# Seven products instead of eight in the input projection, and a multiplication moved to ScalarE

## The chip, the cores and the metric

The kernel runs on one core of one Trainium2 chip. The metric is the device time of one execution in microseconds (us). TensorE (PE) multiplies matrices, VectorE (DVE) and ScalarE (ACT) work on elements, SyncE (SP) issues most of the transfers (DMA). All data are float32. Products on PE take their operands in two parts, `hi` (the value rounded to a shorter format, fp32r) and `lo` (the rest); one product of two numbers is then three products on PE: hi x hi, hi x lo, lo x hi.

## What is computed

Two layers of an encoder with 256 tokens of width 2048. Per layer, cut to what matters here:

```
h = rmsnorm(x, norm_g[l])
proj = h @ w_in[l]                       # 2048 -> 7168 columns
a_x, a_b, a_c, a_g, d_q, d_k, d_v, d_g, m_q, m_g = split(proj)
q = rmsnorm(d_q per head half of 64)     # differential attention, 6 heads
k = rmsnorm(d_k per head half of 64)
v = d_v;  the attention's output is gated by silu(d_g)
...                                      # gated convolution (a_*), cross-attention (m_*)
x = x + concat(y_A, y_D, y_M) @ w_out[l]
```

## The kernel before

The 256 tokens are two row halves of 128 (`NT` = 2). The normalised, transposed input stands in SBUF as `xT`, hi and lo, in 16 row tiles of 128 (`KT`). A projection is worked off in blocks of 512 columns (`NB`). `block` (L308) holds two accumulators in PSUM, one for each row half, and walks the 16 row tiles in chunks of two (`CK`). For a chunk `load_w` (L284) loads 2 x 128 x 512 weights into a `raw` tile (L291, SP's queue), ACT casts `hi` (L294), DVE subtracts `lo` (L295). `products` (L298, L305) then makes 2 row tiles x 2 row halves x 3 parts = 12 products on PE. Four `raw`, four `hi` and four `lo` tiles go round, so the preparation of a chunk can run three chunks ahead of its products. The PSUM has four banks for accumulators (two blocks), two with the tag `s` and two with the tag `t`.

The six blocks of the differential attention begin at column `C_D`: blocks 0 to 2 are queries and keys, blocks 3 to 5 values and gates. Layer 0 takes them in the order 0 to 5. Layer 1 begins blocks 3 and 0 with the first 12 row tiles, ends them when the last quarter of the new x is there, and goes on with 1, 2, 4, 5. After each of blocks 0 to 2 `normed_steps` (L427) makes the norm's factors: squares on ACT (L436), sums on DVE (L437), an inverse square root as a chain of small DVE steps (`rsqrt`, L192), and then one DVE multiplication for each row half that writes the scaled block into a sheet (L445). The sheet is turned by DVE (L481) and carried through DRAM by DMA.

Work beside the blocks is written as generators. `run_side` counts the chunks and steps each generator when its count has come; `later(g, n)` starts one n chunks on. The order of an engine's instructions is made when the program is built, by a scheduler that puts each as early as its inputs allow, in the order of the program where several are ready. `pin` (`keep_in_program_order`) ties an instruction behind the one that the program issued just before it on the same engine.

In the output projection a scheme with seven products is already used, for two blocks of 512 columns at once and a pair of row tiles. `token_sums` (L353) makes four sums of token tiles on DVE, with their hi and lo. `seven` (L368) loads two rows of tiles of 1024 columns into `wide` tiles (L373), makes sums and differences of weights on DVE (L380) and their hi and lo (L377), and makes seven products of three parts each (L351): into the accumulators of the `near` and the `far` block, and into four more banks `x1`, `x5`, `x6`, `x7` (tags `s` and `t`). `collect` adds these up on DVE when the last pair has been made (L1247, L1251). Layer 0 has two such pairs there, layer 1 three.

Of the kernel before, what the change touches and what calls it, by code (L numbers as in the profile page):

```python
# [10 lines left out]
F32 = mybir.dt.float32  # L11
F32R = mybir.dt.float32r
I32 = mybir.dt.int32
AF = mybir.ActivationFunctionType
ALU = mybir.AluOpType
# [3 lines left out]
P = 128  # L19
# [3 lines left out]
NT = SEQ // P  # L23
# [6 lines left out]
HALF = 64  # L30
MH = W_MEM // P
EPS = 1e-6
NB = 512
CK = 2
PARTS = 8
SPLIT = 3
B = 32
NA = P // B
PAIR_EVERY = 9
QT = NB // P  # L40
# [3 lines left out]
C_D = 3072  # L44
# [4 lines left out]
def encoder(ctx: ExitStack, tc: tile.TileContext, x, mem, norm_g, w_in, conv_w, conv_b,  # L49
            dq_g, dk_g, lq1, lk1, lq2, lk2, head_g, mem_norm_g, w_mem_kv, mq_g, mk_g, w_out, out):  # L50
    nc = tc.nc
# [9 lines left out]
    keep = pool("keep", 1)  # L61
# [9 lines left out]
    def nm(s):  # L71
        uid[0] += 1
        return f"{s}_{uid[0]}"
# [140 lines left out]
    def later(g, n):  # L214
        due[id(g)] = chunk[0] + n
        return g
# [55 lines left out]

        return w[k * P:(k + CK) * P].rearrange("(j p) c -> p j c", p=P)

    def x_row_tiles(w, k):

        q, j = divmod(k, QT)
        return w[q * NB:(q + 1) * NB].rearrange("(p j) c -> p j c", j=QT)[:, j:j + CK]

    def raw_tile():  # L280
        return wp.tile([P, CK, NB], F32, tag="raw", name=nm("raw"), bufs=4)
# [16 lines left out]
    def accumulators():  # L298
        return [ps_acc.tile([P, NB], F32, tag="acc", name=nm("acc")) for _ in range(NT)]
# [53 lines left out]
    def token_sums(stat, k, home):  # L353

        f = tmp.tile([P, 2, SEQ], F32, tag="nat", name=nm("f"), bufs=3)
        pin(nc.vector.tensor_tensor(f, stat[:, 0, k:k + 2, :].bitcast(F32), stat[:, 1, k:k + 2, :].bitcast(F32), ALU.add))
        a11, a21, a12, a22 = f[:, 0, 0:P], f[:, 0, P:SEQ], f[:, 1, 0:P], f[:, 1, P:SEQ]
        s = tmp.tile([P, 4, P], F32, tag="nat", name=nm("sums"), bufs=3)
        yield 1
        pin(nc.vector.tensor_tensor(s[:, 0], a21, a22, ALU.add))  # L360
        pin(nc.vector.tensor_tensor(s[:, 2], a11, a21, ALU.subtract))
        pin(nc.vector.tensor_tensor(s[:, 1], s[:, 0], a11, ALU.subtract))
        pin(nc.vector.tensor_tensor(s[:, 3], a12, s[:, 1], ALU.subtract))
        yield 1
        pin(nc.scalar.copy(home[:, 0], s))
        pin(nc.vector.tensor_tensor(home[:, 1], s, home[:, 0].bitcast(F32), ALU.subtract))

    def seven(stat, k, sums, w, col0, c_near, c_far, x, first, last, homes, meanwhile):  # L368


        a, b = (pl.tile([P, 2, NB], F32, tag=tag, name=nm("wide")) for pl, tag in homes)
        for j, raw in enumerate((a, b)):
            pin(nc.sync.dma_start(raw.rearrange("p j c -> p (j c)"), w[(k + j) * P:(k + j + 1) * P, col0:col0 + 2 * NB]))  # L373

        def split(src, to=None):
            hi, lo = to or parts_tiles()
            return ((hi, pin(nc.scalar.copy(hi, src))), (lo, pin(nc.vector.tensor_tensor(lo, src, hi.bitcast(F32), ALU.subtract))))  # L377

        def minus(dst, v, u):
            pin(nc.vector.tensor_tensor(dst, v, u, ALU.subtract))  # L380

        def side_of(parts, j):
            return [v[:, j] for v, _ in parts]

        one = keep.tile([P, 2, 1, NB], F32R, tag="mga", name=nm("one"))
        b11 = split(a[:, 0:1], (one[:, 0], one[:, 1]))
        minus(a[:, 0], a[:, 1], a[:, 0])
        minus(a[:, 1], b[:, 1], a[:, 1])
        b2 = split(b)
        minus(b[:, 1], b[:, 1], a[:, 0])  # L390
        minus(b[:, 0], b[:, 0], b[:, 1])
        meanwhile()
        t13 = split(a)
        t42 = split(b)

        def tokens(j, t):
            return [stat[:, part, k + j, t * P:(t + 1) * P] for part in range(2)]

        def summed(i):
            return [sums[:, part, i] for part in range(2)]  # L400

        x1, x5, x6, x7 = x
        product(tokens(0, 0), x1, side_of(b11, 0), first, last)
        product(tokens(1, 0), c_near[0], side_of(b2, 0), False, False)
        product(summed(3), c_far[0], side_of(b2, 1), first, False)
        product(summed(0), x5, side_of(t13, 0), first, last)
        product(summed(2), x7, side_of(t13, 1), first, last)
        product(tokens(1, 1), c_near[1], side_of(t42, 0), False, False)
        product(summed(1), x6, side_of(t42, 1), first, last)
# [20 lines left out]
    def normed_steps(vec, acc, gs, st, home):  # L430

        ng = NB // gs
        ss = small.tile([P, NT, ng], F32, tag=f"ss{ng}", name=nm("ss"))
        for t in range(NT):
            sq = tmp.tile([P, NB], F32, tag="nat", name=nm("sq"), bufs=3)
            nc.scalar.activation(sq, acc[t], AF.Square)  # L436
            vec.tensor_reduce(ss[:, t], sq.rearrange("p (g d) -> p g d", d=gs), AX.X, ALU.add)  # L437
            vec.tensor_scalar(ss[:, t], ss[:, t], col(st, R2_64 if gs == HALF else R2_128, t), EPS,
                              ALU.mult, ALU.add)
        r = rsqrt(ss.rearrange("p t g -> p (t g)"), NT * ng, vec).rearrange("p (t g) -> p t g", t=NT)  # L440
        both = home()
        for t in range(NT):
            vec.tensor_scalar(r[:, t], r[:, t], col(st, R, t), None, ALU.mult)
            w = min(gs // B, NA)
            vec.tensor_tensor(  # L445
                both[:, :, :, t].rearrange("p (g b) j c -> p j g b c", b=w),
                acc[t].rearrange("p (j g b c) -> p j g b c", g=NA // w, b=w, c=B),
                r[:, t].rearrange("p (j g) -> p j g", g=NA // w).unsqueeze(3).unsqueeze(4)
                .to_broadcast([P, NB // P, NA // w, w, B]), ALU.mult)
        return both  # L450

    def normed(acc, gs, st, home):
# [595 lines left out]
    for l in range(DEPTH):  # L1048
# [8 lines left out]
        def x_block(cols, order=ALLK, **how):  # L1057
            return block(xT, w_in[l], cols, order, rows=x_row_tiles, **how)

        def begin_pair(n, p):  # L1060
            tasks.append(later(p, max(1, start + round(PAIR_EVERY * n) - chunk[0])))


        order = range(6) if l == 0 else (3, 0, 1, 2, 4, 5)
        begun = {b: x_block([(C_D + b * NB, NB)], ALLK[:-QT], more=True) for b in order[:2]} if l > 0 else {}
        for b in order:
            if b in begun:
                acc = x_block([(C_D + b * NB, NB)], ALLK[-QT:], acc=begun[b])
            else:
                acc = x_block([(C_D + b * NB, NB)], ready=m.ready if l == 0 and b == order[0] else None)  # L1070
            if b == 3:
                v = keep.tile([P, NT, W_DIFF], F32, tag="v", name=nm("v"))
                ga = keep.tile([P, NT, W_DIFF], F32, tag="ga", name=nm("ga"))
            if b == 4:
                start = chunk[0]
                for n in range(DH // 2):
                    begin_pair(n + n // 2 * 2 / 3, pair((2 * n, 2 * n + 1), (lambda heads: diff_scores(l, heads, yT),
                                                                 lambda h, s: diff_weights(l, h, s)),
                                       (lambda h, yn, po, iv: diff_out(h, yn, po, iv, st, ga),
                                        lambda h, y: split_T(yT, CG + h, y, hgain[:, l:l + 1], pin=True)), v))  # L1080
            if b < 3:
                tasks.append(later(qk_T(l, yT, normed(acc, HALF, st, sheets(("mqT", "mga", "e")[b])),
                                 (0, 0, 4) if b == 0 else (0, 4, 2) if b == 1 else None,
                                 (256, 0, 2) if b == 1 else (0, 2, 4) if b == 2 else None), 8))
            else:
                for t in range(NT):
                    if b == 3:
                        nc.scalar.activation(v[:, t, 0:NB], acc[t], AF.Copy, scale=col(st, R, t))
                    elif b == 4:
                        nc.scalar.activation(v[:, t, NB:768], acc[t][:, 0:256], AF.Copy, scale=col(st, R, t))  # L1090
                        silu2(ga[:, t, 0:256], acc[t][:, 256:512], st, t)
                    else:
                        silu2(ga[:, t, 256:768], acc[t], st, t)
# [172 lines left out]

        def pair_at(n):
            def run(near):
                seven(yT, paired[n], sums[n], w_out[l], 2 * NB, near, far, x, n == 0, n == len(paired) - 1,
                      homes[n], (lambda: leave(1, accs[1], pin, 4)) if n == 0 else lambda: None)  # L1270
                if n == len(paired) - 1:
                    tasks.append(later(collect(near), 5))
                run_side(1)
            return run
# [36 lines left out]
```

## Time and profile before

| what | value |
|---|---|
| median of 3 runs | 918.87 us (918.57 to 920.05) |
| profiled execution | 919.19 us |
| its span (first to last instruction) | 917.4 us |
| granted clock of TensorE | 1.00 |
| PE busy | 911.1 us, 99% |
| DVE busy | 712.2 us, 78% |
| ACT busy | 492.8 us, 54% |

A row of a group reads: line, engine, operation, output<-inputs, shapes, count | busy time in us, mean of one in ns | idle time of the engine just before them, and what ended it. A row of a timeline begins with the start and the duration in us and ends, in brackets, with the idle time before it and its releaser. Matmuls overlap, so their busy time says little; the distance of their starts does.

### The profile page before, as it was taken

The page shows a single profiled execution, that of the slowest core. Times are in us where ns is not written, and L with a number is a line of the kernel's source. Part 1 is how long each engine was busy: PE and PEld are TensorE (multiplying, and loading weights), DVE is VectorE, ACT ScalarE, POOL GpSimd, SP SyncE. Part 2 cuts the span into 40 slices and gives each one's busy share as a digit, 9 for nine tenths or more (in the row PEclk, how much of TensorE's full clock was granted, in tenths as well). Part 3 has the DMA queues.
Part 4 walks back from the last instruction along what each step waited for, and adds up shares of the span by engine and source line. Part 5 has one row for each costly group of instructions (what it writes and reads, how often), then busy time and mean ns, then how long its engine had stood idle before and what let it go on. Part 6 is the DMA issues. An engine that isn't in the chain of part 4 may idle for free.

```text
span 917.4 us, 12473 instructions
## 1 busy us (share of the span) xinstructions
PE 911.1 (99%) x4209; PEld 753.6 (82%) x4209; DVE 712.2 (78%) x1281; ACT 492.8 (54%) x770; POOL 38.2 (4%) x68
## 2 busy tenths in 40 slices
PE   8999999999999999999999999999999999999998
PEld 6888888888888888888888888888888888888887
DVE  5579978757789779587689857778888889488786
ACT  5667644445546556445556544456545546446352
POOL 2434010000000000000000000000000000000000
PEclk9999999999999999999999999999999999999999
DMA  8889888885786998989777867997887998978842
GB/s 288 287 245 251 283 247 232 250 235 179 205 235 172 263 273 248 234 248 255 242 220 227 277 196 216 267 243 182 237 223 187 249 268 258 257 227 246 280 155 92
DMA packets 244560, 215.16 MB, mean 235 GB/s; under 512 B 131976, under 2 KB 171720, under 8 KB 244496
## 3 DMA queue, kind: packets, MB, share of 16 engines
q1 hardware_dynamic: 239520, 208.71, 79.0%
q0 software_dynamic: 3776, 4.59, 2.1%
q10 hardware_dynamic: 1200, 1.07, 0.4%
q8 instruction: 33, 0.54, 0.2%
q14 instruction: 31, 0.25, 0.1%
HBM read 193.30 MB, written 21.00 MB: 234 GB/s over the span
## 4 chain that ended last, share of the span: by engine, by line
PE 98%; DMA 1%; SPq 0%; DVE 0%; ACT 0%; issue 0%; ACTq 0%
PE acc L305 91%; PE x L351 2%; PE po L519 1%; PE acc L351 1%; PE s L609 1%; DMA raw<-in_w_mem_kv_dram 1%; PE po L734 1%; PE pt L748 0%; SPq L818 0%; PE s L667 0%; PE s L666 0%; PE s L668 0%; SPq L881 0%; DVE lo L901 0%; DVE lo L295 0%; ACT hi L900 0%
## 5 line engine op out<-in xcount | busy, mean ns | idle before, releaser
L305 PE MATMUL acc<-hi,xT 128*128 128x512 f32 x1792 | 559.5, 390 | 0.0
L294 ACT CAST hi<-raw 128x1024 fp32r<-128x1024 f32 x270 | 283.1, 1052 | 292.3 <-PE acc L305 227.6
L295 DVE TENSOR_TENSOR lo<-raw,hi 128x1024 fp32r<-128x1024 f32 x270 | 328.7, 1220 | 134.8 <-ACT hi L294 133.2
L305 PEld LDWEIGHTS acc<-hi,xT 128*128 128x128 f32 x1792 | 336.2, 188 | 70.0
L305 PE MATMUL acc<-lo,xT 128*128 128x512 f32 x896 | 349.3, 390 | 0.4 <-DVE lo L295 0.4
L305 PEld LDWEIGHTS acc<-lo,xT 128*128 128x128 f32 x896 | 168.2, 188 | 34.3 <-DVE lo L295 0.8
L305 PE MATMUL acc<-hi,yT 128*128 128x512 f32 (+1 forms) x432 | 134.2, 388 | 0.0
L305 PEld LDWEIGHTS acc<-hi,yT 128*128 128x128 f32 x432 | 81.0, 188 | 16.7
L305 PE MATMUL acc<-lo,yT 128*128 128x512 f32 x216 | 83.7, 388 | 0.0
L305 PE MATMUL acc<-hi,memT 128*128 128x512 f32 x248 | 78.1, 393 | 0.0
L305 PEld LDWEIGHTS acc<-hi,memT 128*128 128x128 f32 x248 | 46.1, 188 | 9.5
L901 DVE SCALAR_TENSOR_TENSOR lo<-raw,cva,hi 128x1024 fp32r<-128x1024 f32 (+1 forms) x34 | 41.0, 1218 | 14.6 <-ACT hi L900 14.5
L305 PE MATMUL acc<-lo,memT 128*128 128x512 f32 x124 | 48.0, 391 | 0.3 <-DVE lo L901 0.2
L305 PEld LDWEIGHTS acc<-lo,yT 128*128 128x128 f32 x216 | 40.6, 188 | 8.4
L900 ACT ACTIVATE hi<-raw,cva 128x1024 fp32r<-128x1024 f32 (+1 forms) x34 | 36.5, 1099 | 12.1 <-DMA raw<-in_w_mem_kv_dram 11.9
L623 ACT ACTIVATE e<-e,mx 128x256 f32<-128x256 f32 x48 | 23.8, 497 | 8.4 <-DVE mx L619 8.4
L305 PEld LDWEIGHTS acc<-lo,memT 128*128 128x128 f32 x124 | 23.3, 188 | 6.0 <-DVE lo L901 1.1
L377 ACT CAST hi<-wide 128x1024 fp32r<-128x1024 f32 x15 | 15.5, 1049 | 16.3 <-DVE wide L380 6.8
L765 POOL DMA_DIRECT2D xt<-in_x_dram x32 | 21.4, 677 | 19.4 <-DVE rsy L189 13.9
L377 DVE TENSOR_TENSOR lo<-wide,hi 128x1024 fp32r<-128x1024 f32 x15 | 18.1, 1220 | 3.5 <-ACT hi L377 3.3
L481 DVE STREAM_TRANSPOSE sh<-sh 128x1024 f32<-128x1024 f32 (+2 forms) x14 | 17.3, 1237 | 0.0
L1166 ACT ACTIVATE sh<-acc,st 128x512 f32<-128x512 f32 (+1 forms) x16 | 8.9, 579 | 14.6 <-DMA d<-sh 11.7
(202 smaller groups left out, 713.2 us busy)
## 6 DMA issues: line engine op xcount, KB each, us to landing
raw<-in_w_in_dram SPq DMA_DIRECT2D x192, 512.0 KB, 4.7
raw<-in_w_out_dram SPq DMA_DIRECT2D x54, 512.0 KB, 4.7
raw<-in_w_in_dram SPq DMA_DIRECT2D x64, 256.0 KB, 4.1
raw<-in_w_mem_kv_dram SPq DMA_DIRECT2D x30, 512.0 KB, 6.2
d<-sh SPq DMA_DIRECT2D x88, 128.0 KB, 4.1
sh<-d SPq DMA_DIRECT2D x72, 128.0 KB, 4.3
wide<-in_w_out_dram SPq DMA_DIRECT2D x10, 512.0 KB, 6.6
xs<-in_x_dram SPq DMA_DIRECT2D x4, 512.0 KB, 6.5
```

Source lines behind the costliest of these rows:

```text
L294: nc.scalar.copy(hi, raw)
L295: nc.vector.tensor_tensor(lo_, raw, hi.bitcast(F32), ALU.subtract)
L305: i = nc.tensor.matmul(acc, left, right, start=start, stop=stop)
L351: nc.tensor.matmul(acc, left[a], right[b], start=first and i == 0, stop=last and i == 2)
L377: return ((hi, pin(nc.scalar.copy(hi, src))), (lo, pin(nc.vector.tensor_tensor(lo, src, hi.bitcast(F32), ALU.subtract))))
L481: tc.keep_in_program_order(nc.vector.transpose(src, src))
L519: nc.tensor.matmul(po[:, t, :], eT[:, i, t, k, :], v[:, k, h * P:(h + 1) * P], start=k == 0, stop=k == NT - 1)
L609: pin(nc.tensor.matmul(s[c][:, i, :], yT[rows, a, h, i * P:(i + 1) * P], yT[rows, b, CG + h, :], start=n == 0, stop=n == 2))
L623: nc.scalar.activation(e[:, c, i], e[:, c, i], AF.Exp, bias=mx[:, c, i:i + 1], accum_out=sm[:, c, i:i + 1])
L765: tc.keep_in_program_order(nc.gpsimd.dma_start(st[:, n], src[n * B:(n + 1) * B].rearrange("p (b r) -> b p r", b=NA)))
L900: both = (nc.scalar.activation(hi[:, j], raw[:, j], AF.Copy, scale=g), nc.vector.scalar_tensor_tensor(lo[:, j], raw[:, j], g, hi[:, j].bit ...
L901: nc.vector.scalar_tensor_tensor(lo[:, j], raw[:, j], g, hi[:, j].bitcast(F32), ALU.mult, ALU.subtract))
```

## The change

In each layer two blocks of w_in are made together with the scheme of seven products for some of their row tiles: blocks 3 and 4 in layer 0, with one pair of row tiles (0 and 1), put in after four chunks of block 3; blocks 1 and 2 in layer 1, with two pairs (row tiles 0 to 3), put in after three and after five chunks of block 1. The remaining row tiles of both blocks are made as before. `x_sums` makes the token sums of `xT`, in layer 0 right ahead of block 3, in layer 1 right after block 3. `collect` forms four sums `us` in SBUF from the banks of the x tiles, beginning directly behind the last pair, and `gather` adds the accumulators to them when a block ends; what follows reads `us` in place of the accumulators. Homes of new tiles are tags that exist. In blocks 0 to 2 of both layers the multiplication by the norm's factors (`gs == HALF`) goes from two DVE operations of 512 columns to sixteen ACT operations of 64 columns; that of the memory queries stays on DVE.

```diff
-    def x_row_tiles(w, k):
+    def x_row_tiles(w, k, n=CK):
         q, j = divmod(k, QT)
-        return w[q * NB:(q + 1) * NB].rearrange("(p j) c -> p j c", j=QT)[:, j:j + CK]
+        return w[q * NB:(q + 1) * NB].rearrange("(p j) c -> p j c", j=QT)[:, j:j + n]
...
-    def seven(stat, k, sums, w, col0, c_near, c_far, x, first, last, homes, meanwhile):
+    def seven(stat, k, sums, rows, c_near, c_far, x, first, last, homes, meanwhile, single=(keep, "mga")):
...
-            pin(nc.sync.dma_start(raw.rearrange("p j c -> p (j c)"), w[(k + j) * P:(k + j + 1) * P, col0:col0 + 2 * NB]))
+            pin(nc.sync.dma_start(raw.rearrange("p j c -> p (j c)"), rows(k + j)))
...
-        one = keep.tile([P, 2, 1, NB], F32R, tag="mga", name=nm("one"))
+        one = single[0].tile([P, 2, 1, NB], F32R, tag=single[1], name=nm("one"))
...
-            vec.tensor_tensor(
-                both[:, :, :, t].rearrange("p (g b) j c -> p j g b c", b=w),
-                acc[t].rearrange("p (j g b c) -> p j g b c", g=NA // w, b=w, c=B),
-                r[:, t].rearrange(...)..., ALU.mult)
+            to = both[:, :, :, t].rearrange("p (g b) j c -> p j g b c", b=w)
+            of = acc[t].rearrange("p (j g b c) -> p j g b c", g=NA // w, b=w, c=B)
+            if gs == HALF:
+                for at in range(ng):
+                    j, g = divmod(at, NA // w)
+                    nc.scalar.activation(to[:, j, g], of[:, j, g], AF.Copy, scale=r[:, t, at:at + 1])
+            else:
+                vec.tensor_tensor(to, of, r[:, t]..., ALU.mult)
...
+        def x_sums(n, tag):
+            home = keep.tile([P, 2, 4, P], F32R, tag=tag, name=nm("sums"))
+            for _ in token_sums(xT, 2 * n, home):
+                pass
+            return home
+
+        def joint(b, places, summed, home):
+            near, far = accumulators(), accumulators()
+            x = [pl.tile([P, NB], F32, tag=tag, name=nm("x"))
+                 for pl, tag in ((ps_s, "s"), (ps_s, "s"), (ps_t, "t"), (ps_t, "t"))]
+            u = keep.tile([P, 3, NB], F32, tag=home, name=nm("u"))
+            us = [u[:, 0], u[:, 1], u[:, 2], tmp.tile([P, NB], F32, tag="yn", name=nm("u"))]
...
+            def collect():
+                x1, x5, x6, x7 = x
+                pin(nc.scalar.copy(us[0], x1))
+                plus(us[2], us[0], x6)
+                plus(us[1], us[2], x7)
+                yield 1
+                plus(us[2], us[2], x5)
+                plus(us[3], us[1], x5)
+
+            def pair_at(n):
+                def run(near):
+                    rows = lambda k: x_row_tiles(w_in[l], k, 1)[:, 0, C_D + b * NB:C_D + (b + 2) * NB]
+                    seven(xT, 2 * n, summed[n], rows, near, far, x, n == 0, n == len(places) - 1,
+                          ((tmp, ("sh", "e")[n]),) * 2, lambda: None, ((tmp, "e"), (keep, "mga"))[l])
+                    if n == len(places) - 1:
+                        tasks.append(later(collect(), 1))
+                    run_side(1)
+                return run
+
+            x_block([(C_D + b * NB, NB)], ALLK[2 * len(places):], acc=near, opened=(False, False),
+                    between={c: pair_at(n) for n, c in enumerate(places)})
+            return near, far, us
+
+        def gather(acc, us):
+            for t in range(NT):
+                nc.vector.tensor_tensor(us[t], acc[t], us[t], ALU.add)
+            return us
...
+        near_b, far_b, places, tags, home = ((3, 4, (8,), ("bgx",), "bgT"), (1, 2, (6, 10), ("bgT", "mkT0"), "bgx"))[l]
+        far, summed = None, []
         for b in order:
             if b in begun:
                 acc = x_block([(C_D + b * NB, NB)], ALLK[-QT:], acc=begun[b])
+                if b == 3:
+                    for n in range(len(places)):
+                        summed.append(x_sums(n, tags[n]))
+            elif b == near_b:
+                if not summed:
+                    summed = [x_sums(n, tags[n]) for n in range(len(places))]
+                acc, far, us = joint(b, places, summed, home)
+                acc = gather(acc, us[0:2])
+            elif b == far_b:
+                acc = x_block([(C_D + b * NB, NB)], ALLK[2 * len(places):], acc=far, opened=(True, False))
+                acc = gather(acc, us[2:4])
             else:
```

More of the change, by code (lines that the diff above doesn't have):

```diff
@@ L444, in normed_steps @@
             w = min(gs // B, NA)
-            vec.tensor_tensor(
-                both[:, :, :, t].rearrange("p (g b) j c -> p j g b c", b=w),
-                acc[t].rearrange("p (j g b c) -> p j g b c", g=NA // w, b=w, c=B),
-                r[:, t].rearrange("p (j g) -> p j g", g=NA // w).unsqueeze(3).unsqueeze(4)
-                .to_broadcast([P, NB // P, NA // w, w, B]), ALU.mult)
+            to = both[:, :, :, t].rearrange("p (g b) j c -> p j g b c", b=w)
[5 more added lines that the diff above has]
+            else:
+                vec.tensor_tensor(to, of, r[:, t].rearrange("p (j g) -> p j g", g=NA // w).unsqueeze(3).unsqueeze(4)
+                                  .to_broadcast([P, NB // P, NA // w, w, B]), ALU.mult)
         return both
@@ L1058, in x_block, with plus @@
             return block(xT, w_in[l], cols, order, rows=x_row_tiles, **how)
+        def x_sums(n, tag):
[9 more added lines that the diff above has]
+            us = [u[:, 0], u[:, 1], u[:, 2], tmp.tile([P, NB], F32, tag="yn", name=nm("u"))]
+            def plus(dst, v, u):
+                pin(nc.vector.tensor_tensor(dst, v, u, ALU.add))
+            def collect():
[22 more added lines that the diff above has]
+            return us
         def begin_pair(n, p):
@@ L1268, in run @@
             def run(near):
-                seven(yT, paired[n], sums[n], w_out[l], 2 * NB, near, far, x, n == 0, n == len(paired) - 1,
+                seven(yT, paired[n], sums[n], lambda k: w_out[l][k * P:(k + 1) * P, 2 * NB:4 * NB], near, far, x, n == 0, n == len(paired) - 1,
                       homes[n], (lambda: leave(1, accs[1], pin, 4)) if n == 0 else lambda: None)
```

## The prediction

> **What bounds the kernel now.** I read the page's busy table first, then the groups of instructions, then the groups in the stretch that the change touches, then the timelines of VectorE (DVE) and ScalarE (ACT) there.
>
> ```profile
> span 917.4 us, 12473 instructions
> PE 911.1 (99%) x4209; PEld 753.6 (82%) x4209; DVE 712.2 (78%) x1281; ACT 492.8 (54%) x770; POOL 38.2 (4%) x68
> L294 ACT CAST hi<-raw 128x1024 fp32r<-128x1024 f32 x270 | 283.1, 1052 | 292.3 <-PE acc L305 227.6
> L295 DVE TENSOR_TENSOR lo<-raw,hi 128x1024 fp32r<-128x1024 f32 x270 | 328.7, 1220 | 134.8 <-ACT hi L294 133.2
> ...
> L305 PE MATMUL acc<-hi,xT 128*128 128x512 f32 x193 | 59.5, 389 | 0.0
> L305 PE MATMUL acc<-lo,xT 128*128 128x512 f32 x96 | 37.3, 389 | 0.0
> ```
>
> TensorE (PE) is idle for 917.4 - 911.1 = 6.3 us in all. The column behind the second bar shows who waits: ACT's cast of a weight chunk waits 227.6 us for PE to give back a `hi` buffer, and DVE's `lo` waits 133.2 us for ACT. Both helpers run ahead and PE sets the pace. The last two rows are the groups of PE between 549.6 and 614.9 us, three blocks of layer 1: 289 products in 65.3 us, one of them shared with the block before. So a product costs PE 65.3/288 = 0.2267 us (its 389 ns overlap the next), a chunk of two row tiles (12 products) 2.72 us, a block of eight chunks 21.8 us.
>
> How far do the helpers run ahead? These are rows of two timelines in the first block that would be paired, block 3 of layer 0; ACT's first, DVE's behind the dots:
>
> ```profile
> 163.16 1.28 ACT L436 ACTIVATE sq<-acc 128x512 f32<-128x512 f32 x2 [0.98 <-PE acc L305]
> 172.00 1.05 ACT L294 CAST hi<-raw 128x1024 fp32r<-128x1024 f32 x1 [1.66 <-PE acc L305]
> 174.72 1.05 ACT L294 CAST hi<-raw 128x1024 fp32r<-128x1024 f32 x1 [1.15 <-PE acc L305]
> ...
> 163.79 1.37 DVE L437 TENSOR_REDUCE ss<-sq 128x8 f32<-128x512 f32 x2 [0.36 <-ACT sq L436]
> 165.41 1.23 DVE L295 TENSOR_TENSOR lo<-raw,hi 128x1024 fp32r<-128x1024 f32 x1
> 167.65 1.23 DVE L295 TENSOR_TENSOR lo<-raw,hi 128x1024 fp32r<-128x1024 f32 x1
> 170.37 1.23 DVE L295 TENSOR_TENSOR lo<-raw,hi 128x1024 fp32r<-128x1024 f32 x1 [0.36 <-ACT hi L294]
> 171.78 1.28 DVE L445 TENSOR_TENSOR sh<-acc,rsy 128x512 f32<-128x512 f32 x2
> 173.09 1.22 DVE L295 TENSOR_TENSOR lo<-raw,hi 128x1024 fp32r<-128x1024 f32 x1
> ```
>
> A buffer given back at 172.00 holds a finished `lo` at 173.09 + 1.22 = 174.31. PE then still has three prepared chunks, until 172.00 + 3 x 2.72 = 180.16. The lead is 5.9 us: DVE may fall that far behind before PE feels it.
>
> **Part 1, the products removed.** A pair replaces 2 row tiles x 2 row halves x 2 blocks x 3 parts = 24 products by 7 x 3 = 21. Three pairs remove 9: 9 x 0.2267 = **2.04 us**, all on the path. No product is added elsewhere (sums and collecting are DVE's and ACT's), so this is the most that can be gained.
>
> **Part 2, what DVE gets.** The same scheme already runs five times on w_out, so its prices stand in rows by shape:
>
> ```profile
> L377 DVE TENSOR_TENSOR lo<-wide,hi 128x1024 fp32r<-128x1024 f32 x15 | 18.1, 1220 | 3.5 <-ACT hi L377 3.3
> L377 DVE TENSOR_TENSOR one<-wide,one 128x512 fp32r<-128x512 f32 x5 | 3.4, 683 | 0.0
> L380 DVE TENSOR_TENSOR wide<-wide 128x512 f32<-128x512 f32 x10 | 6.9, 692 | 0.3
> L356 DVE TENSOR_TENSOR f<-yT 128x512 f32<-128x512 f32 x5 | 3.4, 684 | 0.0
> L360 DVE TENSOR_TENSOR sums<-f 128x128 f32<-128x128 f32 x5 | 1.4, 284 | 0.0
> L366 DVE TENSOR_TENSOR sums<-sums,sums 128x512 fp32r<-128x512 f32 x5 | 3.4, 683 | 0.0
> L1247 DVE TENSOR_TENSOR u<-u,x 128x512 f32<-128x512 f32 x8 | 5.2, 676 | 0.1
> L445 DVE TENSOR_TENSOR sh<-acc,rsy 128x512 f32<-128x512 f32 x16 | 10.2, 681 | 0.0
> ```
>
> A pair: 3 x 1.220 + 0.683 + 4 x 0.692 = 7.11 us of DVE, in 21 x 0.2267 = 4.76 us of PE. The two ordinary chunks that it replaces cost 2 x 1.22. Token sums: 0.684 + 4 x 0.284 + 0.683 = 2.50 us a pair. Collecting and gathering: 8 additions of 0.676 a layer, 5.4 us. Given back: 12 multiplications of 0.681 (the 16 of the row less the four of the memory queries), 8.2 us. Sum over the kernel: 3 x (7.11 - 2.44 + 2.50) + 2 x 5.4 - 8.2 = +24 us of DVE, on 712.2 of 917.4. On average that is hidden; locally it may not be:
>
> ```profile
> 543.70:549.60 5.90, 5.90 (x28) 4.89 (x27) 2.91 (x3) 3.36 (x4) 0.00 (x0) 1.00 0.64 178
> 549.60:571.40 21.80, 21.80 (x97) 18.04 (x97) 15.82 (x29) 9.53 (x11) 0.00 (x0) 1.00 0.74 219
> 571.40:593.10 21.70, 21.70 (x97) 17.98 (x96) 16.86 (x30) 10.46 (x11) 0.00 (x0) 1.00 0.96 264
> 457.40:485.70 28.30, 28.30 (x125) 23.29 (x125) 25.54 (x29) 18.27 (x28) 0.00 (x0) 1.00 0.72 219
> ```
>
> Columns: stretch, length, busy PE, PEld, DVE, ACT, POOL, clock (1.00 throughout), DMA share and GB/s.
>
> *Layer 0* (one pair, after four chunks of block 3, which begins at T0 = 163.1). PE reaches the pair at T0 + 10.9. Its third product needs the sums at T0 + 10.9 + 6 x 0.2267 = T0 + 12.2, its sixth the last difference (`t42`) at T0 + 10.9 + 15 x 0.2267 = T0 + 14.3. From 163.79 (T0 + 0.7) DVE owes: the norm of block 2, which took from 163.79 to 171.78 with three `lo` inside it, 8.0 - 3.7 = 4.3 us; one `lo`, 1.22; the pair, 7.11; the sums, 2.50, pinned behind the norm's last DVE step. That is 15.1 us, done at T0 + 15.8: **0 to 1.5 us** late, zero if ready products of the next chunk fill the place.
>
> *Layer 1* (two pairs in block 1, after three and five chunks; T0 = 549.6). Both sums, 5.0 us, fall due in the 5.9 us before T0, where DVE is idle for 3.0: 2.0 spill over. With the norm of block 0 (4.3) and the pair (7.11) they end at T0 + 13.4, and the first pair's sixth product wants them at T0 + 3 x 2.72 + 15 x 0.2267 = T0 + 11.6: 1.8 late. Over the whole block DVE has 15.82 - 2 x 1.22 + 2 x 7.11 + 4 x 0.676 (collecting) - 1.36 (moved) + 2.0 = 30.9 us of work in 6 x 2.72 + 2 x 4.76 = 25.8 us of PE, 5.1 behind at its end, of a lead of 5.9. Block 2 gives it back: 16.86 - 2.44 + 1.35 - 1.36 = 14.4 in 16.3. So **0 to 1.8 us**.
>
> Lost on PE: 0 to 3.3 us. The nearest row is the stretch 457.4 to 485.7, two pairs of w_out beside transposes and residual additions: DVE 25.54 of 28.30, PE idle for nothing. There DVE finished the last differences only when PE was in the pair:
>
> ```profile
> 466.94 2.36 DVE L377 TENSOR_TENSOR lo<-wide,hi 128x1024 fp32r<-128x1024 f32 x2 [1.79 <-ACT hi L377]
> ...
> 466.98 0.86 PE L351 MATMUL x<-one,yT 128*128 128x512 f32 x3
> 470.65 0.39 PE L351 MATMUL x<-hi,sums 128*128 128x512 f32 x1
> 470.87 0.39 PE L305 MATMUL acc<-hi,yT 128*128 128x512 f32 x1
> 471.10 0.39 PE L351 MATMUL acc<-lo,yT 128*128 128x512 f32 x1
> ```
>
> The order of products has the next chunk's between the pair's (470.87), and no gap opened. I take **0.9 us**, nearer to that row than to 3.3, because it is 90% load there against 30.9/25.8 = 120% here.
>
> **Part 3, what ACT gets.** Sixteen small multiplications a block, six blocks.
>
> ```profile
> L1088 ACT ACTIVATE v<-acc,st 128x512 f32<-128x512 f32 x4 | 2.7, 691 | 2.0 <-PE acc L305 2.0
> L1090 ACT ACTIVATE v<-acc,st 128x256 f32<-128x256 f32 x4 | 1.9, 476 | 2.0 <-PE acc L305 2.0
> 206.68 0.48 ACT L1090 ACTIVATE v<-acc,st 128x256 f32<-128x256 f32 x1 [0.99 <-PE acc L305]
> 207.05 0.47 ACT L508 ACTIVATE th<-acc,st 128x256 f32<-128x256 f32 x1
> ```
>
> From 256 to 512 elements the same operation grows by 215 ns, 0.84 ns an element; 64 elements come to 476 - 192 x 0.84 = 315 ns. Starts lie 0.37 apart for 0.48, so each follows the last after about 0.2 us: 16 x 0.2 = 3.3 us of ACT in place of 1.36 of DVE. A cast of the next chunk behind them in ACT's queue comes 3.3 us late at most, inside the lead of 5.9: nothing by itself. Bounds: a gain through DVE is in part 2 already; a loss of up to 3.3 is a rival below.
>
> The Trainium skill speaks against this move: "ScalarE: Activation LUTs", "Rules for kernel authors", wants multiplications on VectorE. Its "What ACT_TABLE_LOAD costs" gives about 280 ns + 0.833 ns an element for an operation with one pointer operand, less 93 ns of overlap: by estimate 240 ns each, 3.8 us a block. By that the burst still lies inside the lead, and the sum would be the same.
>
> **Part 4, queues and waits.** Each pair puts two loads of 512 KB on SP's queue in place of two of 512 KB, and they land later:
>
> ```profile
> raw<-in_w_in_dram SPq DMA_DIRECT2D x192, 512.0 KB, 4.7
> wide<-in_w_out_dram SPq DMA_DIRECT2D x10, 512.0 KB, 6.6
> ```
>
> Their homes (`sh`, `e`) have been idle since the turning of x, so they wait for no buffer; queued behind them are the next `raw` loads and the sheets' carries. Layer 1's stretch ran DMA at 0.74, the next at 0.96 which now has two chunks less. Zero; if the cover were gone, 1.9 us a pair. New waits: `collect` on DVE waits for the pair's last product, and behind it stand the next `lo`s; these are unpinned, so I count them ahead of it. `gather` waits for the block's end and delays the norm by 1.35 us, while the accumulators' next users are a block away. The far accumulators, needed in the near block's middle, wait for the moved multiplications.
>
> **Sum.** Profiled execution 919.19 (span 917.4 and 1.8 around it) - 2.04 + 0.9 = 918.05. It stands 0.32 above the median 918.87 of the runs shown, so against the median: **917.7 us**, -0.12%. What a measurement of this kernel can tell from no change is about 0.2%, 1.84 us.
>
> **Rivals.**
> *Nothing is lost* (0.34). For: five pairs on w_out show no gap on PE. Against: none of them stands beside a norm. 918.87 - 2.04 = 916.8, faster by 0.22%; it needs losses under 0.2 us.
> *ACT's burst joins DVE's lag* (0.09). The sixteen operations of block 2, then of block 0, come just when the pair's casts are due; 5.1 of the lead is spent in layer 1, so 3.3 - (5.9 - 5.1) = 2.5 us are lost there: 917.7 + 2.5 - 0.9 = 919.3, no change. Against: ACT has 9.53 of 21.80 busy.
> *Sums come late* (0.22). In layer 0 they are pinned behind the norm, a chain of small steps between which DVE's order lets longer ones slip (the three `lo` above). If all 7.11 us of the pair slip in, the sums are the last of DVE's 15.1 us and end at T0 + 15.8, against T0 + 12.2: 3.6 us, and four of the seven products hang on them. With 1.8 in layer 1: 918.87 - 2.04 + 3.6 + 1.8 = 922.2. It decides from losses of 3.9 us (2.04 + 1.84) on. For: DVE at 120%; against: next chunk's products can fill 2.7 us.
> *My forecast*, losses of 0.2 to 2.5: 0.35.
>
> So faster 0.34, same 0.35 + 0.09 = 0.44, slower 0.22. The range takes the full saving and 0.3 of scatter below (916.5), and above the larger part of the slow rival (921.5); beyond lie some 0.2. The forecast's own range is 917.0 to 919.3.
>
> **What would show it.** PE: 9 products fewer, the pitch 0.2267 kept; a gap around 174 to 178 us with `sums` as its releaser means the slow rival; gaps near 558 to 572 with `lo<-wide` or `lo<-raw` mean DVE's load; with `hi` behind `sh<-acc,rsy` on ACT, the burst. L445 falls from 16 to 4 on DVE, and 96 small ones of about 315 ns stand on ACT. I am wrong if PE's idle time grows by over 3 us, or if the time falls by more than 2.04 and the scatter.

## The result: 0.45% slower, and the profile after

| | before | after |
|---|---|---|
| median of 11 runs each | 918.75 us | 922.52 us |
| ratio, 95% interval | | 1.0045 (1.0034 to 1.0056) |
| profiled execution | 919.19 us | 922.03 us |

917.7 us was forecast, between 916.5 and 921.5. The time moved the other way, by 3.8 us, and lies above the range.

The page of the changed kernel, its busy table and the two helper groups:

```profile
span 920.3 us, 12620 instructions
PE 912.1 (99%) x4200; PEld 752.4 (82%) x4200; DVE 732.2 (80%) x1321; ACT 518.8 (56%) x877; POOL 38.2 (4%) x68
L294 ACT CAST hi<-raw 128x1024 fp32r<-128x1024 f32 x264 | 275.8, 1053 | 256.7 <-PE acc L305 176.3
L295 DVE TENSOR_TENSOR lo<-raw,hi 128x1024 fp32r<-128x1024 f32 x264 | 320.4, 1220 | 110.6 <-ACT hi L294 108.8
```

PE has 9 instructions fewer, as worked out, and DVE is busy for 20 us more (24 were worked out). ACT's wait for PE has fallen from 227.6 to 176.3 us, but that is no measure of the loss: it is 171.6 us in a kernel further down that is not slower than before (two operations in place of sixteen). Nor does PE's idle time show the loss: it grew from 6.3 to 8.2 us only. The starts of PE's products do. The timeline of PE around layer 0's pair:

```profile
174.63 0.86 PE L351 MATMUL x<-one,xT 128*128 128x512 f32 x3
175.33 0.39 PE L351 MATMUL acc<-hi,xT 128*128 128x512 f32 x1
175.56 0.40 PE L351 MATMUL acc<-hi,sums 128*128 128x512 f32 x1
177.56 0.74 PE L351 MATMUL x<-hi,sums 128*128 128x512 f32 x2 [1.60 <-ACT hi L377]
178.14 0.40 PE L351 MATMUL acc<-lo,xT 128*128 128x512 f32 x1
...
178.84 0.39 PE L351 MATMUL acc<-hi,sums 128*128 128x512 f32 x1
180.15 0.50 PE L351 MATMUL acc<-hi,xT 128*128 128x512 f32 x1 [0.92 <-ACT hi L377]
```

Starts that should lie 0.227 us apart lie 2.00 and 1.31 apart: 1.77 + 1.08 = 2.85 us lost, against 0.68 saved by this pair (3 products). The releaser is not `sums`, as the slow rival wanted, but the pair's own casts on ACT. ACT's timeline just before:

```profile
164.90 1.04 ACT L294 CAST hi<-raw 128x1024 fp32r<-128x1024 f32 x1
169.67 3.38 ACT L450 ACTIVATE sh<-acc,rsy 128x64 f32<-128x64 f32 x16 [3.73 <-DVE rsy L443]
172.82 0.74 ACT L377 CAST one<-wide 128x512 fp32r<-128x512 f32 x1
173.33 1.18 ACT L377 CAST hi<-wide 128x1024 fp32r<-128x1024 f32 x1
174.28 0.74 ACT L365 CAST sums<-sums 128x512 fp32r<-128x512 f32 x1
176.46 1.04 ACT L377 CAST hi<-wide 128x1024 fp32r<-128x1024 f32 x1 [1.44 <-DVE wide L380]
179.05 1.04 ACT L377 CAST hi<-wide 128x1024 fp32r<-128x1024 f32 x1 [1.54 <-DVE wide L380]
```

The pair's loads were issued at 158.3 and 158.8 and landed within 5.8 us. ACT was idle from 165.9 to 169.7. Yet the first cast, `one`, came at 172.82: in ACT's order it stands behind the sixteen multiplications of block 2, and these wait for that block's norm. From there the pair's preparation is a chain of casts and differences that hand over to each other, and DVE shows how long it is:

```profile
171.12 0.29 DVE L363 TENSOR_TENSOR sums<-f,sums 128x128 f32<-128x128 f32 x1
173.59 0.69 DVE L377 TENSOR_TENSOR one<-wide,one 128x512 fp32r<-128x512 f32 x1 [2.17 <-ACT one L377]
174.31 0.69 DVE L380 TENSOR_TENSOR wide<-wide 128x512 f32<-128x512 f32 x1
...
178.85 2.50 DVE L377 TENSOR_TENSOR lo<-wide,hi 128x1024 fp32r<-128x1024 f32 x2
```

DVE idles 2.17 us for `one`, then works until 181.35: 8.5 us from the first cast to the last `lo`, while PE reaches the pair at 174.63. In layer 1 the first pair is early enough; the second meets the burst of block 0:

```profile
565.09 0.62 ACT L377 CAST one<-wide 128x512 fp32r<-128x512 f32 x1
565.61 3.37 ACT L450 ACTIVATE sh<-acc,rsy 128x64 f32<-128x64 f32 x16
568.76 2.10 ACT L377 CAST hi<-wide 128x1024 fp32r<-128x1024 f32 x2
```

To split the loss by layer I use the last ScalarE scaling of the convolution (L1166, now L1227; the first row half), late in each layer's projection. Layer 0's, before and after, then layer 1's:

```profile
420.26 0.48 ACT L1166 ACTIVATE sh<-acc,st 128x256 f32<-128x256 f32 x1 [0.94 <-PE acc L305]
...
422.67 0.48 ACT L1227 ACTIVATE sh<-acc,st 128x256 f32<-128x256 f32 x1 [0.94 <-PE acc L305]
...
827.85 0.48 ACT L1166 ACTIVATE sh<-acc,st 128x256 f32<-128x256 f32 x1 [0.94 <-PE acc L305]
...
830.68 0.48 ACT L1227 ACTIVATE sh<-acc,st 128x256 f32<-128x256 f32 x1 [0.94 <-PE acc L305]
```

Layer 0 is 2.41 us late, and next to nothing of it stood before the pair: by 163.1 us, where block 3 begins, PE had started 709 products in both kernels, although the squares of block 2 begin 0.56 us later after the change. Layer 1 adds 0.42 where it should have given back 1.36, so it loses some 1.8 us too, in smaller pieces. Counted by the starts on PE they are 0.2 us in its first pair, 0.5 in the second, 0.4 near 625 us, where 24 small products of the attention come as 2 and 22, 0.2 between 633 and 645 us, and 0.5 between 680 and 700 us. The last piece is lost in every kernel with layer 1's pairs.

### The profile page after: what moved, and what is told of

Same layout as the page of the kernel before. It is cut to its first block, busy times and chain, and to the rows that moved or that the text cites. A ratio compares the mean times of both kernels' runs of the same rounds, so it can differ in the third digit from the quotient of the medians.

```text
span 920.3 us, 12620 instructions
## 1 busy us (share of the span) xinstructions
PE 912.1 (99%) x4200; PEld 752.4 (82%) x4200; DVE 732.2 (80%) x1321; ACT 518.8 (56%) x877; POOL 38.2 (4%) x68
## 4 chain that ended last, share of the span: by engine, by line
PE 90%; DMA 3%; DVE 2%; ACT 2%; issue 1%; SPq 1%; POOL 0%; DVEq 0%; ACTq 0%
PE acc L305 82%; PE x L351 2%; PE acc L351 1%; DMA d<-sh 1%; DMA raw<-in_w_mem_kv_dram 1%; PE po L523 1%; PE s L613 1%; DVE lo L905 1%; ACT sh L450 1%; PE po L738 1%; PE acc L922 1%; DMA sh<-d 0%; ACT hi L377 0%; ACT hi L294 0%; DMA xt<-in_x_dram 0%
## 5 line engine op out<-in xcount | busy, mean ns | idle before, releaser
L305 PE MATMUL acc<-hi,xT 128*128 128x512 f32 x1744 | 545.5, 390 | 0.0
L294 ACT CAST hi<-raw 128x1024 fp32r<-128x1024 f32 x264 | 275.8, 1053 | 256.7 <-PE acc L305 176.3
L295 DVE TENSOR_TENSOR lo<-raw,hi 128x1024 fp32r<-128x1024 f32 x264 | 320.4, 1220 | 110.6 <-ACT hi L294 108.8
L305 PEld LDWEIGHTS acc<-hi,xT 128*128 128x128 f32 x1744 | 327.1, 188 | 68.2
L305 PE MATMUL acc<-lo,xT 128*128 128x512 f32 x872 | 340.1, 390 | 0.1
L305 PEld LDWEIGHTS acc<-lo,xT 128*128 128x128 f32 x872 | 163.8, 188 | 33.6 <-DVE lo L295 1.0
L377 ACT CAST hi<-wide 128x1024 fp32r<-128x1024 f32 x24 | 25.1, 1063 | 24.5 <-DVE wide L380 13.0
L377 DVE TENSOR_TENSOR lo<-wide,hi 128x1024 fp32r<-128x1024 f32 x24 | 29.1, 1221 | 5.4 <-ACT hi L377 5.1
L351 PE MATMUL x<-hi,sums 128*128 128x512 f32 x48 | 17.7, 395 | 1.6 <-ACT hi L377 1.6
```

The source lines that it names most:

```text
L294: nc.scalar.copy(hi, raw)
L295: nc.vector.tensor_tensor(lo_, raw, hi.bitcast(F32), ALU.subtract)
L305: i = nc.tensor.matmul(acc, left, right, start=start, stop=stop)
L351: nc.tensor.matmul(acc, left[a], right[b], start=first and i == 0, stop=last and i == 2)
```

## The experiments

Theory A: the sixteen multiplications cost only where a pair's casts stand behind them. Theory B: VectorE is overloaded wherever pairs stand. Rivals C and D: ScalarE's time costs by itself. Each kernel was timed 5 to 12 times against before on its own chip (before: 918.8 to 918.9).

**One part alone.** In the table of blocks, a layer's entry is replaced by `(None, None, (), (), None)`, for both layers in the third kernel; in the fourth `if gs == HALF:` becomes `if False:`.

> Only layer 0's pair and the multiplications on ScalarE; layer 1's blocks as before (6 row-tile products more than the full change). Theory A (the loss sits in layer 0: its pair's first cast stands on ScalarE behind the sixteen small multiplications): most of the loss stays, 2.0 to 3.5 us over before, about 921.5, with the same gap of about 2.0 + 1.1 us of TensorE between 175 and 180 us. Theory B (VectorE is overloaded wherever pairs stand, worst in layer 1): under 1 us over before.

> Only layer 1's two pairs and the multiplications on ScalarE. Theory A: the gap at 175 us is gone; 6 products of 0.2267 are saved (1.36 us) and about 0.6 lost in slower starts and a small gap, so 0 to 1.3 us below before, about 918. Theory B: layer 1 is the overloaded place, so at least 2 us over before.

> No pairs at all, only the multiplications by the norm's factors on ScalarE. Theory A: the burst of 3.3 us lies inside the lead of 5.9 us, so no change (within 0.5 us of before). Rival C (ScalarE's bursts delay the casts of ordinary chunks by themselves): over 1 us slower, with gaps on TensorE whose releaser is the cast hi<-raw.

> All three pairs, but the multiplications stay on VectorE. Theory A: layer 0's first cast no longer waits for sixteen ScalarE operations, only for the first VectorE multiplication, about 3 us earlier; the gaps of 3 us near 175 to 180 shrink by more than half, the whole is 1 to 2 us below the full change. Theory B: VectorE has 8.2 us more to do, the time rises by 1 us or more over the full change.

| kernel | median us | ratio to before (95%) |
|---|---|---|
| layer 0's pair only | 921.30 | 1.0026 (1.0018 to 1.0035) |
| layer 1's pairs only | 920.01 | 1.0010 (1.0001 to 1.0019) |
| multiplications on ACT only, no pair | 918.71 | 0.9998 (0.9990 to 1.0007) |
| all pairs, multiplications on DVE | 918.41 | 0.9996 (0.9988 to 1.0005) |

The move to ScalarE alone costs nothing, the pairs without it cost nothing (though they don't bring the 2.04 us either), and both together cost 3.8 us: it is their meeting. Theory B falls: 8.2 us more of DVE work made the kernel 4.1 us faster. Theory A had expected only 1 to 2 us from the fourth kernel, and a gain from layer 1 alone; both layers lose. In the fourth kernel the pair's first cast runs 7 us earlier on ACT (165.85 for 172.82), ahead of the multiplications on DVE; DVE still takes its part of `one` only behind them, 2.1 us earlier than after the change (171.50 for 173.59), and of the two gaps 0.48 us remain. ACT's row, then DVE's:

```profile
165.85 0.62 ACT L377 CAST one<-wide 128x512 fp32r<-128x512 f32 x1
...
169.70 1.28 DVE L452 TENSOR_TENSOR sh<-acc,rsy 128x512 f32<-128x512 f32 x2
```

**Moving the pair away from the burst.** The first two kernels are the full change with one of these edits each. The third has the second edit and `if False:`, the fourth layer 1's pairs alone and `if False:`.

```diff
-  ((tmp, "e"), (keep, "mga"))[l])
+  ((keep, "ga"), (keep, "mga"))[l])       # casts ahead of the burst
```
```diff
-  ((3, 4, (8,), ("bgx",), "bgT"), ...
+  ((3, 4, (12,), ("bgx",), "bgT"), ...    # six chunks, not four
```

> The full change, but layer 0's single part lives in the tag ga and not in e, so that the scheduler no longer holds the pair's first cast until the sheet of block 2 (also e) has begun: in ScalarE's order the pair's four casts now stand ahead of the sixteen multiplications. Theory A' (ScalarE's order makes the loss): the gap of 2.0 us for hi<-wide at 175 us goes; but the norm's chain, and behind it the token sums, now come after the pair's differences, so TensorE waits for the sums instead, 1 to 3 us: total 919.5 to 922. Theory D (it is the 3.3 us of ScalarE time itself, wherever it stands): about 922.5 as the full change.

> The full change, with layer 0's pair after six chunks of block 3 and not after four (5.4 us later). Theory A (the pair meets the norm of block 2 and its burst of multiplications): both are over, the gaps at 175 to 180 us go, and layer 0 gains its 0.68 us; the total falls by 2.5 to 3.2 us to about 919.5. Theory B (load of VectorE over the block): the work is the same, so the time stays within 1 us of the full change's 922.5.

> Multiplications back on VectorE and layer 0's pair after six chunks. Theory A: the remaining gap of layer 0 (0.5 us at 177 us with the multiplications on VectorE) goes too: 0.3 to 1 us below that kernel, about 917.7, and below before. Theory B: no difference to the kernel with the multiplications on VectorE, 918.4.

> Only layer 1's pairs, multiplications on VectorE. Theory A (in layer 1 too the burst stands ahead of the second pair's casts, and costs about 1 us): about 1 us below the kernel with layer 1's pairs and the multiplications on ScalarE, which measured 920.0: about 919. Theory B: VectorE at 120% of the block: 8.2 us more of VectorE work make it slower than 920.0.

| kernel | median us | ratio to before (95%) |
|---|---|---|
| tag `ga`, casts ahead of the burst | 921.65 | 1.0027 (1.0017 to 1.0037) |
| pair after six chunks | 921.66 | 1.0029 (1.0018 to 1.0040) |
| DVE, pair after six chunks | 917.42 | 0.9988 (0.9978 to 0.9997) |
| layer 1's pairs only, DVE | 918.19 | 0.9995 (0.9986 to 1.0004) |

The first shows why `one` stood behind the burst: it shares the tag `e` with the sheet that the burst writes. In another tag it runs first, and the burst and the sums come last. The shared tag holds no buffer back: in the kernel with the multiplications on DVE, `one` has it too, and runs ahead of the sheet (165.85 and 169.70 above). What it does is set an order, which cost time here where both stood in ACT's queue. Why the scheduler orders them so was not looked into. ACT's timeline of the kernel with the tag `ga`, then PE's:

```profile
164.85 0.62 ACT L377 CAST one<-wide 128x512 fp32r<-128x512 f32 x1
165.68 1.05 ACT L377 CAST hi<-wide 128x1024 fp32r<-128x1024 f32 x1 [0.21 <-PE acc L305]
...
176.37 3.40 ACT L450 ACTIVATE sh<-acc,rsy 128x64 f32<-128x64 f32 x16 [0.95 <-DVE rsy L443]
179.53 0.74 ACT L365 CAST sums<-sums 128x512 fp32r<-128x512 f32 x1
...
178.45 0.40 PE L305 MATMUL acc<-hi,xT 128*128 128x512 f32 x1
180.32 0.50 PE L351 MATMUL acc<-hi,sums 128*128 128x512 f32 x1 [1.48 <-ACT sums L365]
```

This is the slow rival of the prediction, norm late and sums last, with a gap of 1.6 us: it exists, but only once the casts are out of the way. The later place missed its 919.5: the burst moved along with the norm's chain, from 169.67 to 173.59, and the casts still stood behind it. The pair moved further, from 174.63 to 181.37, and PE loses only 0.4 us at it (21 products in 5.14 us for 4.76). But the two chunks behind it wait for `lo` on VectorE, 1.0 us in all. ACT's rows, then one of PE's waits:

```profile
173.59 3.40 ACT L450 ACTIVATE sh<-acc,rsy 128x64 f32<-128x64 f32 x16 [1.85 <-DVE rsy L443]
176.75 0.74 ACT L377 CAST one<-wide 128x512 fp32r<-128x512 f32 x1
...
190.83 0.50 PE L305 MATMUL acc<-lo,xT 128*128 128x512 f32 x1 [0.50 <-DVE lo L295]
```

With the multiplications on DVE the same place leaves no gap at layer 0's pair. The time is 0.12% below before, the best version found, and 1 us below the fourth kernel, though the two intervals overlap. Layer 1 alone gains 1.8 us from taking the burst away (920.01 to 918.19), where 1 was expected.

**Burst only where it meets a pair, only where it doesn't, and earlier sums.** A flag in `normed_steps`, set ahead of each norm; the sums of layer 0 at the start of block 2:

```diff
-            if gs == HALF:
+            if gs == HALF and spread[0]:
...
+            spread[0] = b != (2, 0)[l]      # apart;  == for together
             if b < 3:
```
```diff
+            if l == 0 and b == 2:           # early, with the tag ga
+                summed = [x_sums(n, tags[n]) for n in range(len(places))]
```

> All three pairs; the multiplications stay on VectorE only in the two norms that meet a pair (block 2 of layer 0, block 0 of layer 1) and go to ScalarE in the other four. Theory A (the burst costs only where the pair's casts stand behind it): nearly the whole loss goes, within 0.7 us of the kernel with all multiplications on VectorE, 918.4. Theory D (ScalarE time anywhere costs): two of six bursts gone, one third of the 4.1 us between the two kernels, about 921.

> The reverse: multiplications on ScalarE only in the two norms that meet a pair, on VectorE in the other four. Theory A: the loss is that of the full change, 921.5 to 923. Theory D: one third of it, about 919.8.

> The full change with layer 0's single part in the tag ga and its token sums made one block earlier, so that neither the casts nor the sums stand behind the norm and its burst. What still stands behind them is the release of block 2's accumulators, which the far block needs. Theory A: the gap for the sums (1.9 us at 178 us with the casts alone moved) shrinks below 1 us, and the total comes to 919 to 920.5, layer 1's burst being left. If the release of the accumulators ends last, a gap of over 1.5 us at the first far product takes its place and the total stays near 921.5.

> As the kernel with the two meeting norms on VectorE, and layer 0's pair after six chunks. Theory A: no gap over 0.3 us in layer 0 and 0.3 to 1.5 us below before, about 917.5, level with the kernel that has all multiplications on VectorE and this place (917.4); a candidate for the best version.

| kernel | median us | ratio to before (95%) |
|---|---|---|
| four bursts apart from pairs | 918.94 | 1.0008 (0.9999 to 1.0017) |
| two bursts that meet a pair | 921.73 | 1.0034 (1.0021 to 1.0046) |
| tag `ga`, sums a block earlier | 919.98 | 1.0019 (1.0008 to 1.0031) |
| apart, pair after six chunks | 917.80 | 0.9992 (0.9983 to 1.0001) |

Two bursts of six carry most of the loss: 921.73 against 918.41 with none, 3.3 of the 4.1 us. The other four cost 0.5 us (918.94), and 0.4 with the later place (917.80 against 917.42). That fits theory A, and not D. The small rest has a place in the traces: in both kernels with four bursts the 24 small products near 622 us again come as 2 and 22, 0.4 us longer than in one group, and in the kernels without sixteen operations in layer 1's blocks 1 and 2 they don't. With casts and sums both out of the burst's way, layer 0's gap shrinks to 0.34 us.

**Length or order?** Two operations of 512 columns in place of sixteen of 64; and layer 0's pair alone with neither burst nor early place. The first kernel leaves out seven of the eight factors of each row half, so it serves for its time alone.

```diff
-                for at in range(ng): ... nc.scalar.activation(to[:, j, g], of[:, j, g], AF.Copy, scale=r[:, t, at:at + 1])
+                nc.scalar.activation(<all of t>, <all of acc[t]>, AF.Copy, scale=r[:, t, 0:1])
```

> The full change, but each row half's multiplication on ScalarE is one operation of 512 columns with the first group's factor, in place of eight of 64 (the factors of the other seven groups are left out). The first cast of layer 0's pair still stands behind the norm. Theory A1 (the length of the burst is the loss): the burst falls from 3.3 to 1.4 us; about two thirds of the loss go, 918.5 to 920. Theory A2 (standing behind the norm is the loss, however short the burst): 921.5 or more.

> Only layer 0's pair, after six chunks, multiplications on VectorE. Theory A: no gap, the full 3 products saved, 0.68 us: about 918.1 against before at 918.8. Theory B (VectorE's extra work of the pair costs by itself): 919 or more.

Measured: 917.48 (0.9987, 0.9978 to 0.9996) and 918.53 (0.9999, 0.9990 to 1.0008). ACT's timeline of the first, then PE's at the pair:

```profile
170.71 0.69 ACT L448 ACTIVATE sh<-acc,rsy 128x512 f32<-128x512 f32 x1 [3.73 <-DVE rsy L443]
171.29 0.61 ACT L377 CAST one<-wide 128x512 fp32r<-128x512 f32 x1
171.81 1.04 ACT L377 CAST hi<-wide 128x1024 fp32r<-128x1024 f32 x1
172.75 0.68 ACT L448 ACTIVATE sh<-acc,rsy 128x512 f32<-128x512 f32 x1
...
177.04 0.40 PE L351 MATMUL acc<-hi,sums 128*128 128x512 f32 x1
177.28 0.62 PE L351 MATMUL x<-hi,sums 128*128 128x512 f32 x2
177.74 0.39 PE L351 MATMUL acc<-lo,xT 128*128 128x512 f32 x1
```

`one` still stands behind the norm, 0.58 us after the first multiplication instead of 3.15, and PE has no gap at the pair. So what decides is how long the operations ahead of `one` take, not the waiting for the norm. Theory A1 had expected two thirds of the loss to go, 918.5 to 920; all of it went. `one` now stands behind one of the two operations only: it follows right behind the first write of the sheet, the shared tag again. All pairs, all sums and all of DVE's additions are in this kernel, and it is 1.35 us faster than before. Layer 0's pair alone is level with before within its interval; its 0.68 us can't be told from nothing.

## Why the prediction was wrong, step by step

- **Part 1 held**: 9 products fewer (4209 to 4200 instructions of PE), and where no burst holds up a pair (917.4, 917.5) 1.35 to 1.5 us of the 2.04 arrive.
- **Part 2 was right in its number by luck.** DVE's growth was 20 us for 24. The kernel with two operations (917.48) and the one with everything on DVE and the later place (917.42) came out near the 917.7 that 0.9 us for DVE's lag gave. But that lag isn't there: with the pairs, sums and additions of the full change on DVE, the kernel with two operations has no gap at a pair. Its three pairs take 0.3 us more than 63 products at 0.2267, and 0.5 us go between 680 and 700 us. In the full change the sum for layer 0 went wrong too: it counted DVE's 15.1 us without a wait, done at T0 + 15.8 = 178.9, and DVE ended at 181.35, after idling 2.17 us for `one`.
- **Part 3 is the step that failed.** The burst's size was right: 3.3 us worked out, 3.38 measured, each operation 0.2 us after the last. "Inside the lead of 5.9: nothing by itself" was right for an ordinary chunk, and the kernel with the move alone shows it. But the lead is measured at `hi<-raw`, one cast prepared three chunks ahead. A pair's preparation is a chain, four casts and eight DVE steps that hand over to each other for 8.5 us, and it began with a cast behind the burst. For that chain the lead is how early it may start, and its start was the end of the burst. The term for the burst was put at nothing; it cost 4.1 us (922.52 against 918.41 with the multiplications on DVE).
- **The rival "ACT's burst joins DVE's lag"** named the mechanism, but placed its loss in layer 1 alone, at 2.5 us, and gave it 0.09. It came in both layers: 2.5 us over before with layer 0's pair alone, 1.2 with layer 1's. "ACT has 9.53 of 21.80 busy" counted as evidence against; an average says nothing of what stands behind what in one queue.
- **Sums come late** had nearly the right time, 922.2, for another reason. The rows show the four sums done at 171.41, ahead of the pair's differences, and PE at the first product with sums (175.56) without a wait; nothing slipped into the norm because the pair's first cast was held back.
- **Part 4**: I read that the homes `sh` and `e` were free, but not that `one` would share `e` with the sheet written by the very operations that were moved. The kernel shows both lines. Transfers were put at zero, and that stays open for layer 1 (below).
- **The Trainium skill**, "ScalarE: Activation LUTs" ("Rules for kernel authors"), wants a multiplication on VectorE. The runs agree where the burst meets a pair (922.52 against 918.41), and show no difference where there is no pair (918.71 against 918.77 before), although sixteen operations took 3.38 us and VectorE's two take 1.28. The 0.2 us between starts is less than the 240 ns that the prediction estimated from the Trainium skill's "What ACT_TABLE_LOAD costs", and the measurement decides.
- **What would show it**: the sign listed for the burst, `hi` behind `sh<-acc,rsy` on ACT, is what the trace has, at the place (174 to 178 us) listed for the sums. The sign of being wrong, PE's idle time up by over 3 us, did not show (1.9 us more), although the time was 3.8 us longer.

Left open: a gap of 0.6 to 1.8 us near 635 us that appears in seven kernels with layer 1's pairs, always with `lo` on VectorE as its releaser, and not in the full change. A candidate is the transfers of weights, which part 4 put at zero. Between 540 and 645 us ACT's casts wait for a `raw` tile to land in every kernel with layer 1's pairs, 3.8 to 15.8 us in all, and not once before the change or in the kernels without these pairs. The row of ACT's waits in the full change (us in total, times, the longest):

```profile
ACT hi L294 <- DMA raw<-in_w_in_dram: 10.8, 9, 2.8
```

That these waits make the gap is not shown: the kernel at 917.42 has 10.6 us of them and no gap. No run was aimed at it; nor are all of layer 1's 1.8 us assigned to single waits.

## What to carry to other kernels

A lead measured on one kind of work doesn't cover another: for a chain of casts and differences that crosses two engines, ask when its first link may start and what stands ahead of it in that engine's queue. Moving work to the emptier engine in many small operations can lengthen the one queue that matters; two operations in place of sixteen were worth 5 us here, though the average load favoured the move. Where two tiles share a tag, the second one's first instruction may be ordered behind the first one's writer; that cost time here because both stood in the queue of one engine.

## What was not expected of the hardware

Some products of a pair start a little farther apart than those of a chunk, 0.23 to 0.24 us for 0.227, without a wait that the profile shows. These are PE's rows in layer 1's first pair, in the kernel with two operations:

```profile
560.50 0.40 PE L351 MATMUL acc<-hi,xT 128*128 128x512 f32 x1
560.73 0.39 PE L351 MATMUL x<-hi,sums 128*128 128x512 f32 x1
560.96 0.39 PE L351 MATMUL x<-lo,sums 128*128 128x512 f32 x1
561.20 0.39 PE L351 MATMUL x<-hi,sums 128*128 128x512 f32 x1
```

In the second pair of the same kernel such products start 0.227 apart (571.75, 571.98, 572.21, 572.43), so it isn't the kind of product alone. Over the three pairs of that kernel it comes to 0.3 us, off a saving of 2.04. Why they do so was not tried.
